# A round of the down projection by seven products for eight, in the middle of the second SwiGLU block

## The chip, the cores and the metric

The kernel runs on one core of a Trainium2 chip. The metric is the device time of one execution in microseconds; of several runs the median counts. A core has a matrix engine (TensorE, PE in the profile), a vector engine (VectorE, DVE), a scalar engine (ScalarE, ACT), GpSimd (POOL), an engine that here only issues transfers (SyncE, SP), and DMA queues. TensorE accumulates into eight PSUM banks; the other engines take results out of them.

## The reference

One decoder layer for 512 tokens of 1024 channels: a SwiGLU block, a mixing block (attention, convolution and memory side by side), and a second SwiGLU block. The change concerns the second SwiGLU block:

```python
def swiglu(x, w_gate, w_up, w_down):
    return (jax.nn.silu(x @ w_gate) * (x @ w_up)) @ w_down
...
        x = x + 0.5 * swiglu(rms_norm(x, g_ffn1[l]), w_ffn1_gate[l], w_ffn1_up[l], w_ffn1_down[l])
...
        x = x + 0.5 * swiglu(rms_norm(x, g_ffn2[l]), w_ffn2_gate[l], w_ffn2_up[l], w_ffn2_down[l])
    return x
```

The hidden width is 2816, which is 22 tiles of 128. Everything is float32.

## The kernel before

**Layout and precision.** x stays in SBUF, turned, as eight pieces [128 channels, 512 tokens]; `x[:, d]` is piece d. Each operand is split into a rounded high part and the rest (hi and lo), and each product is the sum of three matmuls, hi by hi, hi by lo and lo by hi. The high part of a weight is cast by ScalarE (L214, L208), the low part is a subtraction on VectorE (L219, L209).

**A SwiGLU block.** It runs over 22 hidden tiles f. The first few (four in block 1, three in block 2) use plain products; the others use `fast`, which computes the gate and the up projection of a tile by a scheme of seven products instead of eight on halves of 256 tokens: seven blocks of 12 matmuls 128x256, 84 in all, with sums of weights made by VectorE (`make_sums`, L160 to L163) and sums of results made by ScalarE (copies out of PSUM) and VectorE. The gate's sum is at L629, its Silu on ScalarE at L630, the up sum at L640 and their product at L644.

**Rounds of the down projection.** The hidden tiles are gathered in rounds, and each round's contribution is added to x while later tiles are computed. In block 2 the rounds are tiles 0 to 2, 3 to 6, 7 to 10, 11 to 14, 15 to 17 and 18 to 21 (`PLANS`). Round 3, tiles 11 to 14, is spread over tiles 15 to 18: each of them gets one load of down weights and two steps of `down` for two pieces of x, 24 matmuls of 128x256 each, accumulated into x by VectorE at L671. The first step stands ahead of the product B_T4 of `fast`, the second behind the tile's hidden result. The last round, tiles 18 to 21, is done behind tile 21 by `seven(g)`, g = 0 to 3, each for two pieces of x: seven products of six matmuls instead of eight. It needs three parts of a weight as they are, four sums of quarters (`four`, L147 to L150), and sums of the hidden tiles by pairs (`paired`). `seven` leaves its results by L529 (a scaled sum of PSUM and x, then a transfer to the output); half sums of products go through ScalarE (`half`, L515) into s12 and s45, which are added to x by VectorE (L519) or by a GpSimd transfer that accumulates (L521).

**Weights.** `Weights` keeps a list of loads and a list of items to split. Raw loads of 512 KB go through four buffers (wraw) on SP's queue, each issued as soon as the split of the last item that reads the old content of its buffer is done; split weights go through four buffers (w0 to w3), a tile's last item through vhi and vlo. `W.next()` gives the next item and splits up to three ahead.

**What sets the order.** The program order below is given to a scheduler, which orders each engine's instructions by its own estimates of their times; only the last stage (`seven`) keeps the written order. TensorE, ScalarE and VectorE each run their list in order and wait on semaphores. PSUM banks: four `mm`, two `sc`, two `tp`. Work tiles `t`: five; `sum` tiles: three.

Of the kernel before, what the change touches and what calls it, by code (L numbers as in the profile page):

```python
# [85 lines left out]
class Weights:  # L86
# [36 lines left out]
    def add_seven(self, ap, off):  # L123
# [116 lines left out]
class Plan:  # L240
# [12 lines left out]
    def steps(self, f):  # L253

        first, second, third = self.rounds[:3]
        if f < first[1]:
            return [], [], []
        if f < second[1]:
            early = self.loads(0) if self.direct < 4 else self.loads(0)[:-1]
            late = self.loads(0)[len(early) :]  # L260
            return early if f == second[0] else [], late if f == second[0] + 1 else [], []
        queue = [d for q in range(1, self.last) for d in self.loads(q)]
        i = f - third[0]
        if f < NF - 1:
            return [], [queue[i]], []
        return ([], [], queue[i:]) if self.seven else ([], [queue[i]], queue[i + 1 :])


PLANS = {
    1: Plan([(0, 4), (4, 8), (8, 12), (12, 16), (16, 18), (18, 22)], 4, False),  # L270
    2: Plan([(0, 3), (3, 7), (7, 11), (11, 15), (15, 18), (18, 22)], 3, True),
}


def layer(tc, ctx, a):
# [35 lines left out]
    def ffn_weights(n, memory):  # L311
        gu, plan = a[f"wgu{n}"], PLANS[n]

        def down(r, g):
            lo, hi = plan.rounds[r]
            m = plan.per_load(r)
            return a[f"wd{n}"][g * m : (g + 1) * m, :, lo:hi].rearrange("d p k m -> p d (k m)")

        for f in range(NF):
            pre, mid, post = plan.steps(f)  # L320
            for d in pre:
                W.add(down(*d), OTHER if d[0] else WIDE, n == 2 and d[0] == 0)
            if f < plan.direct:
                for i in range(2):
                    W.add(flat(gu[f, i]), WIDE, n == 2 and f > 1)
            else:
                W.add_pair(flat(gu[f, 0]), flat(gu[f, 1]), [(down(*d), OTHER if d[0] else WIDE) for d in mid])
            for d in post:
                W.add(down(*d), OTHER if d[0] else WIDE)
            if memory and f == MEM_F:  # L330
                for t in range(2):
                    W.add(flat(a["wmk"][t]), HALF)
                for c in range(2):
                    W.add(flat(a["wmv"][:, 4 * c : 4 * c + 4]), TURNED)
        r = plan.last
        for g in range(KT // plan.per_load(r)):
            (W.add_seven if plan.seven else W.add)(down(r, g), (HALF, OTHER)[g % 2])

    ffn_weights(1, True)
    for t in range(12):  # L340
# [120 lines left out]
    def ffn(pool, norm, first, gain, hooks, next_gain, last):  # L461
# [3 lines left out]
        W.extra = pool  # L465
        bh, bl = {}, {}

        even, sevens, later = {}, [], []

        def halves(t):  # L470
            hi, lo = (both := atile("h7"))[:, :256], both[:, 256:]
# [4 lines left out]
        def paired(f, t):  # L476

            l, r = t[:, :256], t[:, 256:]
            if not (f - plan.rounds[-1][0]) % 2:
                even[f] = l, r, halves(l)  # L480
                return
            el, er, first = even[f - 1]
            m = pool.tile([P, 4, 256], F32, tag="sum", name=nm("h7"), bufs=SUM_BUFS)
            t1, t2, t3, t4 = (m[:, i] for i in range(4))
            out = [first, halves(l)]
            DVE.tensor_tensor(t1, er, el, op=ALU.subtract)
            out.append(halves(t1))
            DVE.tensor_tensor(t2, r, t1, op=ALU.subtract)
# [6 lines left out]
            sevens.append(out)  # L495

        def seven(g):

# [7 lines left out]
            def prod(ps, w, at, step, block, first):  # L506
                for q in range(2):
                    hi, lo = sevens[q][block]
                    s = slice(at + q * step, at + q * step + P)
                    PE.matmul(ps, w[0][:, s], hi, start=first and q == 0, stop=False, skip_group_check=not first)  # L510
                    PE.matmul(ps, w[0][:, s], lo, start=False, stop=False, skip_group_check=not first)
                    PE.matmul(ps, w[1][:, s], hi, start=False, stop=q == 1, skip_group_check=not first)

            def half(to, ps, sign=1):
                ACT.activation(to, ps, AF.Copy, scale=0.5 * sign)  # L515

            def add(to, part):
                if g > 1:
                    DVE.tensor_tensor(to, to, part, op=ALU.add)  # L519
                else:  # L520
                    POOL.dma_start(to, part, accum_op=ALU.add)  # L521

            def leave(d, t, ps):
                o = work()[:, : t.stop - t.start]
                xd = x[:, d, t]
                if ps.shape[-1] < t.stop - t.start:
                    o, xd = (v.rearrange("p (a b) -> p a b", a=2) for v in (o, xd))
                    ps = ps.unsqueeze(1).to_broadcast([P, 2, 256])
                DVE.scalar_tensor_tensor(o, ps, 0.5, xd, op0=ALU.mult, op1=ALU.add)  # L529
                if len(o.shape) == 3:  # L530
                    o = o.rearrange("p a b -> p (a b)")
# [3 lines left out]
            if g < 2:  # L535
                W.four(W.items[W.at + 4][0])
            wa, ws = W.next(), W.next()
            prod(b, wa, 0, 256, H_11, True)
            half(s12[:, l], b)
            prod(de[:, l], wa, 128, 256, H_21, True)  # L540
            prod(de[:, r], ws, 0, 128, H_T1, True)
            half(s45[:, r], de[:, r])
            while later:
                leave(*later.pop(0))
            prod(b, ws, 256, 128, H_T2, False)
            half(s12[:, r], b)
            add(x0, s12)
            prod(c, wa, 512, 128, H_T4, True)
            half(s45[:, l], c, -1)
            add(x1, s45)  # L550
            W.split_to(W.at + 3)
            prod(de[:, r], ws, 768, 128, H_22, False)
            prod(b, ws, 512, 128, H_T3, False)
            whole = slice(0, T)
            if end:
                leave(2 * g, whole, de)
                leave(2 * g + 1, l, b)
                leave(2 * g + 1, r, b)
            else:
                later.extend([(2 * g + 1, whole, b), (2 * g, whole, de)])  # L560

        def hidden(f, t):
            if plan.seven and f >= plan.rounds[-1][0]:
                paired(f, t)
                return
            h_hi[f], h_lo[f] = atile("hh"), atile("hl")
# [46 lines left out]
        def fast(f, mid):  # L613
# [14 lines left out]
            product(de[:, r], w2, 0, B_22, False)  # L628
            DVE.tensor_tensor(g, de, s12, op=ALU.add)  # L629
            ACT.activation(g, g, AF.Silu)  # L630
# [86 lines left out]
            for hook in hooks.get(f, ()):  # L717
                hook()
        r = plan.last
        if plan.seven:  # L720
# [683 lines left out]
```

## Time and profile before

| | us |
|---|---|
| median of 3 runs | 861.53 (861.43 to 861.96) |
| profiled execution | 861.62 |
| span of the profile | 859.8 |
| granted TensorE clock | 1.0 |
| in_wgu load, issue to landing, median | 3.6 |
| GpSimd accumulating transfer x<-s, 256 KB | 3.8 |

The span runs from the first to the last instruction of the profiled execution; its own time is longer by what lies around it. The page's second part gives the busy share in 40 slices, tenths per slice, 21.5 us each; the second block fills the last fifteen or so:

```profile
PE   8999999999999999999999999999999999999997
DVE  7998977877868897869989985899787878787896
...
DMA  7335334333453434222010323863334342323325
```

TensorE is busy in nearly all of every slice, VectorE in six to nine tenths, the transfers in one to seven.

### The profile page before, as it was taken

To read this page: it belongs to the slowest core of one execution; us is meant where nothing else is said; L and a number is where in the kernel's file an instruction comes from. 1 tells how busy PE (TensorE), PEld (TensorE's weight loads), DVE (VectorE), ACT (ScalarE), POOL (GpSimd) and SP (SyncE) were. 2 spreads that over 40 slices of the span, in tenths; PEclk is the share of its full clock that TensorE was granted. 3 is DMA by queue.
4 is the path that set the end of the run, shared out by engine and by line. 5 is a ranking of instruction groups with operands and counts; after the bars stand their busy time and mean duration, and the time that the engine had idled before them with its cause. 6 is when DMAs were issued, how large, how long until landed. Compare 5 with 4: busy or idle time off the path is not lost. (4 is left out here: it accounts for less than half of the span.)

```text
span 859.8 us, 15853 instructions
## 1 busy us (share of the span) xinstructions
PE 850.1 (99%) x6397; PEld 788.6 (92%) x6397; DVE 708.9 (82%) x1208; ACT 466.3 (54%) x792; POOL 37.4 (4%) x40
## 2 busy tenths in 40 slices
PE   8999999999999999999999999999999999999997
PEld 5889999999999999988676788889999999999997
DVE  7998977877868897869989985899787878787896
ACT  7465555455654444633948764656554544545554
POOL 0000000000000000300000022120000000000001
PEclk9999999999999999999999999999999999999999
DMA  7335334333453434222010323863334342323325
GB/s 274 123 91 149 105 98 125 98 119 127 129 157 120 123 111 130 74 98 62 13 32 31 113 97 100 178 141 122 123 98 124 99 123 86 114 96 103 95 75 148
DMA packets 36795, 95.13 MB, mean 111 GB/s; under 512 B 3441, under 2 KB 8049, under 8 KB 36721
## 3 DMA queue, kind: packets, MB, share of 16 engines
q1 hardware_dynamic: 32032, 85.99, 32.1%
q0 software_dynamic: 3536, 6.55, 4.6%
q10 hardware_dynamic: 1152, 1.57, 0.6%
q8 instruction: 50, 0.82, 0.4%
q14 instruction: 25, 0.20, 0.1%
HBM read 88.07 MB, written 2.10 MB: 105 GB/s over the span
## 5 line engine op out<-in xcount | busy, mean ns | idle before, releaser
L609 PE MATMUL mm<-bh,w 128*128 128x256 f32 x888 | 245.5, 276 | 0.4 <-ACT kept L624 0.4
L610 PE MATMUL mm<-bl,w 128*128 128x256 f32 x888 | 245.2, 276 | 0.0
L611 PE MATMUL mm<-bh,w 128*128 128x256 f32 x888 | 245.2, 276 | 0.0
L609 PEld LDWEIGHTS mm<-bh,w 128*128 128x128 f32 x888 | 166.7, 188 | 0.8 <-ACT kept L624 0.6
L415 PE MATMUL mm<-hl,w 128*128 128x256 f32 (+1 forms) x584 | 167.3, 287 | 0.0
L416 PE MATMUL mm<-hh,w 128*128 128x256 f32 (+1 forms) x584 | 167.2, 287 | 0.0
L414 PE MATMUL mm<-hh,w 128*128 128x256 f32 (+1 forms) x584 | 167.0, 287 | 0.0
L610 PEld LDWEIGHTS mm<-bl,w 128*128 128x128 f32 x888 | 166.7, 188 | 0.1
L611 PEld LDWEIGHTS mm<-bh,w 128*128 128x128 f32 x888 | 166.7, 188 | 0.0
L214 ACT CAST w<-wraw 128x1024 fp32r<-128x1024 f32 (+2 forms) x119 | 119.1, 1005 | 74.8 <-PE mm L611 23.7
L219 DVE TENSOR_TENSOR w<-wraw,w 128x1024 fp32r<-128x1024 f32 (+2 forms) x113 | 132.5, 1176 | 29.9 <-ACT w L214 26.4
L219 DVE TENSOR_TENSOR w<-s,w 128x1024 fp32r<-128x1024 f32 x78 | 95.3, 1222 | 40.3 <-PE mm L611 34.5
L414 PEld LDWEIGHTS mm<-hh,w 128*128 128x128 f32 x584 | 109.6, 188 | 2.4 <-ACT hh L567 0.3
L415 PEld LDWEIGHTS mm<-hl,w 128*128 128x128 f32 x584 | 109.6, 188 | 2.2
L416 PEld LDWEIGHTS mm<-hh,w 128*128 128x128 f32 x584 | 109.6, 188 | 2.1
L214 ACT CAST w<-s 128x1024 fp32r<-128x1024 f32 x78 | 81.9, 1052 | 27.1 <-PE mm L611 20.4
L414 PE MATMUL mm<-xh,w 128*128 128x512 f32 x176 | 69.7, 401 | 0.5 <-ACT xh L425 0.4
L415 PE MATMUL mm<-xl,w 128*128 128x512 f32 x176 | 69.4, 394 | 0.6 <-DVE xl L426 0.5
L416 PE MATMUL mm<-xh,w 128*128 128x512 f32 x176 | 69.1, 393 | 0.0
L630 ACT ACTIVATE t<-t 128x512 f32<-128x512 f32 x37 | 23.4, 633 | 68.3 <-DVE t L629 68.3
L671 DVE SCALAR_TENSOR_TENSOR x<-mm,x 128x512 f32<-128x512 f32 x80 | 54.2, 683 | 2.0 <-PE mm L416 2.0
L214 ACT CAST vhi<-wraw 128x512 fp32r<-128x512 f32 x37 | 23.0, 621 | 42.7 <-PE sc L610 34.7
(290 smaller groups left out, 1496.8 us busy)
## 6 DMA issues: line engine op xcount, KB each, us to landing
wraw<-in_wgu SPq DMA_DIRECT2D x86, 512.0 KB, 3.6
wraw<-in_wd SPq DMA_DIRECT2D x38, 512.0 KB, 3.6
wraw<-in_win SPq DMA_DIRECT2D x12, 512.0 KB, 3.5
wraw<-in_wd SPq DMA_DIRECT2D x8, 384.0 KB, 3.3
x<-t POOLq DMA_DIRECT2D x8, 256.0 KB, 4.1
out<-t SPq DMA_DIRECT2D x7, 256.0 KB, 2.3
x<-in_xT SPq DMA_DIRECT2D x3, 512.0 KB, 6.8
wraw<-in_wout_a SPq DMA_DIRECT2D x6, 256.0 KB, 2.7
```

Source lines behind the costliest of these rows:

```text
L214: nc.scalar.copy(hi[:, :cols], raw[:, :cols])
L219: nc.vector.tensor_tensor(lo[:, :cols], raw[:, :cols], hi[:, :cols].bitcast(F32), op=ALU.subtract)
L414: PE.matmul(ps[:, t], wh[:, w], hi(k)[:, t], start=one, stop=False, skip_group_check=cut > 1)
L415: PE.matmul(ps[:, t], wh[:, w], lo(k)[:, t], start=False, stop=False, skip_group_check=cut > 1)
L416: PE.matmul(ps[:, t], wl[:, w], hi(k)[:, t], start=False, stop=end, skip_group_check=cut > 1)
L609: PE.matmul(ps, wh[:, c], bh[k][:, block], start=one, stop=False, skip_group_check=not first)
L610: PE.matmul(ps, wh[:, c], bl[k][:, block], start=False, stop=False, skip_group_check=not first)
L611: PE.matmul(ps, wl[:, c], bh[k][:, block], start=False, stop=end, skip_group_check=not first)
L630: ACT.activation(g, g, AF.Silu)
L671: DVE.scalar_tensor_tensor(o, ps, 0.5, xd, op0=ALU.mult, op1=ALU.add)
```

## The change

Round 3 of block 2 is done by seven products too. `Plan.seven` becomes a tuple of rounds. In tiles 15 to 18 the two `down` steps are replaced by `inside(n, g)`: its first part (`begin`: H_11, H_21, H_T1, 18 matmuls) stands where the first step stood, its second (`end`: H_T2, H_T4, H_22, H_T3, 24 matmuls) behind the hidden result. VectorE adds two results to x from PSUM, and GpSimd issues two transfers that add s12 and s45. The load of 512 KB stays, but becomes two items (three parts; four sums). The hidden tiles 11 to 14 go through `paired`, in which the halves of the even tile are now made with the odd tile. In `fast`, in both blocks, the product B_T3, the second use of the third weight, moves ahead of the first down step and of B_T4. In `seven` the additions for g = 1 go to VectorE, and the last pair (g = 3) is written in another order, with H_21 in a bank of its own.

```diff
@@ add_pair @@
-        for ap, off in mid:
-            self.add(ap, off)
+        for ap, off, seven in mid:
+            (self.add_seven if seven else self.add)(ap, off)
@@ PLANS @@
-    2: Plan([(0, 3), (3, 7), (7, 11), (11, 15), (15, 18), (18, 22)], 3, True),
+    2: Plan([(0, 3), (3, 7), (7, 11), (11, 15), (15, 18), (18, 22)], 3, (3, 5)),
@@ paired @@
-            if not (f - plan.rounds[-1][0]) % 2:
-                even[f] = l, r, halves(l)
+            n = seven_at[f]
+            if not (f - plan.rounds[n][0]) % 2:
+                even[f] = l, r
                 return
-            el, er, first = even[f - 1]
+            el, er = even[f - 1]
...
-            out = [first, halves(l)]
+            out = [halves(el), halves(l)]
@@ new, with product7, half and twice moved out of seven @@
+        def inside(n, g):
+            l, r = slice(0, 256), slice(256, 512)
+            b, de = mm_bank()[:, l], mm_bank()
+            c = sc_bank()[:, l]
+            s12, s45 = work(), work()
+            x0, x1 = x[:, 2 * g], x[:, 2 * g + 1]
+            wa, ws = W.next(), W.next()
+            def begin():
+                product7(b, wa, 0, 256, H_11, True, n)
+                half(s12[:, l], b)
+                product7(de[:, l], wa, 128, 256, H_21, True, n)
+                product7(de[:, r], ws, 0, 128, H_T1, True, n)
+                half(s45[:, r], de[:, r])
+            def end():
+                product7(b, ws, 256, 128, H_T2, False, n)
+                half(s12[:, r], b)
+                product7(c, wa, 512, 128, H_T4, True, n)
+                half(s45[:, l], c, -1)
+                product7(de[:, r], ws, 768, 128, H_22, False, n)
+                product7(b, ws, 512, 128, H_T3, False, n)
+                DVE.scalar_tensor_tensor(x0, de, 0.5, x0, op0=ALU.mult, op1=ALU.add)
+                x2 = x1.rearrange("p (a b) -> p a b", a=2)
+                DVE.scalar_tensor_tensor(x2, twice(b), 0.5, x2, op0=ALU.mult, op1=ALU.add)
+                POOL.dma_start(x0, s12, accum_op=ALU.add)
+                POOL.dma_start(x1, s45, accum_op=ALU.add)
+            return [begin, end]
@@ seven, add @@
-                if g > 1:
+                if g > 0:
                     DVE.tensor_tensor(to, to, part, op=ALU.add)
@@ seven, g = 3 alone (p2: H_21 into bank e; p4: H_T4; p7: H_T3; p3: H_22) @@
             prod(b, wa, 0, 256, H_11, True)
             half(s12[:, l], b)
             prod(de[:, r], ws, 0, 128, H_T1, True)
             half(s45[:, r], de[:, r])
             while later:
                 leave(*later.pop(0))
+            p4()
             prod(b, ws, 256, 128, H_T2, False)
             half(s12[:, r], b)
             add(x0, s12)
+            p2()
+            leave(2 * g, l, e)
+            p7()
+            leave(2 * g + 1, whole, b)
+            p3()
+            leave(2 * g, r, de[:, r])
@@ fast @@
             ACT.activation(g, g, AF.Silu)
+            product(b, w2, 512, B_T3, False)
             rest = []
             for d in mid:
-                rest += down(*d)
+                rest += (inside if d[0] in plan.seven else down)(*d)
             if rest:
                 rest.pop(0)()
             w3 = W.next()
             product(c, w3, 0, B_T4, True)
             ACT.copy(s45[:, l], c)
-            product(b, w2, 512, B_T3, False)
```

The names in the following rows are numbered by load and item: wraw146 is the 146th load, w207 the 207th item, s12 and s43 the sums of two neighbouring loads (gate and up of one tile), s7 the four sums of a down load, t the gate and up sums. On VectorE, at the gate's sum of tile 16 of block 2, there stands before:

```order
L219 TENSOR_TENSOR w206_8536<-wraw142_8356,w206_8536 128x1024
L219 TENSOR_TENSOR w207_8561<-s12_142_8555,w207_8561 128x1024
L629 TENSOR_TENSOR t_788_8474<-mm_784_8470,kept_786_8472 128x512
L160 TENSOR_TENSOR s12_145_8738<-wraw146_8564 128x512
L163 TENSOR_TENSOR s43_145_8739<-wraw145_8539,wraw146_8564 128x512
L161 TENSOR_TENSOR s12_145_8738<-wraw145_8539,s12_145_8738 128x512
L671 SCALAR_TENSOR_TENSOR x_69<-mm_790_8566,x_69 128x512
```

and with the change, at the same place:

```order
L688 TENSOR_TENSOR t_799_8523<-mm_795_8519,kept_797_8521 128x512
L219 TENSOR_TENSOR w208_8626<-wraw142_8433,w208_8626 128x1024
L148 TENSOR_TENSOR s7_144_8754<-s7_144_8754,wraw144_8530 128x256
L149 TENSOR_TENSOR s7_144_8754<-wraw144_8530,s7_144_8754 128x256
L219 TENSOR_TENSOR w209_8637<-s12_142_8631,w209_8637 128x1024
L160 TENSOR_TENSOR s12_145_8827<-wraw146_8640 128x512
L699 TENSOR_TENSOR t_800_8524<-kept_798_8522,mm_794_8518 128x512
L219 TENSOR_TENSOR vlo213_8788<-wraw143_8444,vhi213_8787 128x512
L703 TENSOR_TENSOR t_800_8524<-t_800_8524,t_799_8523 128x512
```

wraw142 and wraw146 use the same buffer. The split that frees it (w206 before, w208 now) stood ahead of the split of s12 and of the gate's sum, and now stands behind the gate's sum (L688); L160, the first sum of wraw146, stands three places behind that split before and four places behind it now.

On ScalarE, from the gate's Silu of the same tile on, there stands before:

```order
L630 ACTIVATE t_788_8474<-t_788_8474 128x512
L214 CAST vhi210_8689<-wraw143_8381 128x512
L638 COPY kept_787_8473<-sc_785_8471 128x256
L214 CAST w208_8592<-s43_142_8556 128x1024
L567 CAST hh_791_8622<-t_789_8475 128x512
```

and now:

```order
L689 ACTIVATE t_799_8523<-t_799_8523 128x512
L214 CAST w209_8637<-s12_142_8631 128x1024
L508 ACTIVATE t_804_8624<-mm_801_8621 128x256
L508 ACTIVATE t_805_8625<-mm_802_8622 128x256
L214 CAST vhi213_8787<-wraw143_8444 128x512
```

The half sums that read the products of `inside` out of PSUM (L508) stand behind the Silu and the cast of the sum s12; before, the cast of that sum stood ahead of the Silu.

On VectorE, the last nine operations before:

```order
L519 TENSOR_TENSOR x_69<-x_69,s12_874_9761 128x512
L519 TENSOR_TENSOR x_69<-x_69,s45_875_9762 128x512
L529 SCALAR_TENSOR_TENSOR t_883_9845<-tp_871_9758,x_69 128x512
L529 SCALAR_TENSOR_TENSOR t_884_9848<-tp_872_9759,x_69 128x512
L519 TENSOR_TENSOR x_69<-x_69,kept_881_9823 128x512
L519 TENSOR_TENSOR x_69<-x_69,t_882_9824 128x512
L529 SCALAR_TENSOR_TENSOR t_885_9879<-mm_879_9821,x_69 128x512
L529 SCALAR_TENSOR_TENSOR t_886_9882<-mm_878_9820,x_69 128x256
L529 SCALAR_TENSOR_TENSOR t_887_9885<-mm_878_9820,x_69 128x256
```

and now:

```order
L558 TENSOR_TENSOR x_69<-x_69,s12_894_9849 128x512
L558 TENSOR_TENSOR x_69<-x_69,s45_895_9850 128x512
L568 SCALAR_TENSOR_TENSOR t_904_9928<-tp_891_9846,x_69 128x512
L568 SCALAR_TENSOR_TENSOR t_905_9931<-tp_892_9847,x_69 128x512
L558 TENSOR_TENSOR x_69<-x_69,t_902_9912 128x512
L558 TENSOR_TENSOR x_69<-x_69,kept_901_9911 128x512
L568 SCALAR_TENSOR_TENSOR t_906_9956<-mm_903_9913,x_69 128x256
L568 SCALAR_TENSOR_TENSOR t_907_9965<-mm_898_9908,x_69 128x512
L568 SCALAR_TENSOR_TENSOR t_908_9974<-mm_899_9909,x_69 128x256
```

Before, three results (one of 512, two of 256) stood together at the end; now the left half, the whole piece and the right half stand one behind the other, each for another product.

More of the change, by code (lines that the diff above doesn't have):

```diff
@@ L326, in ffn_weights @@
             else:
-                W.add_pair(flat(gu[f, 0]), flat(gu[f, 1]), [(down(*d), OTHER if d[0] else WIDE) for d in mid])
+                W.add_pair(flat(gu[f, 0]), flat(gu[f, 1]), [(down(*d), OTHER if d[0] else WIDE, d[0] in plan.seven) for d in mid])
             for d in post:
@@ L336, in ffn_weights @@
         for g in range(KT // plan.per_load(r)):
-            (W.add_seven if plan.seven else W.add)(down(r, g), (HALF, OTHER)[g % 2])
+            (W.add_seven if r in plan.seven else W.add)(down(r, g), (HALF, OTHER)[g % 2])
     ffn_weights(1, True)
@@ L466, in ffn @@
         bh, bl = {}, {}
-        even, sevens, later = {}, [], []
+        even, sevens, later = {}, {r: [] for r in plan.seven}, []
+        seven_at = {f: r for r in plan.seven for f in range(*plan.rounds[r])}
         def halves(t):
@@ L494, in paired, with product7, half, twice @@
             out.append(halves(r))
-            sevens.append(out)
+            sevens[n].append(out)
+        def product7(ps, w, at, step, block, first, n):
+            for q in range(2):
+                hi, lo = sevens[n][q][block]
+                s = slice(at + q * step, at + q * step + P)
+                PE.matmul(ps, w[0][:, s], hi, start=first and q == 0, stop=False, skip_group_check=not first)
+                PE.matmul(ps, w[0][:, s], lo, start=False, stop=False, skip_group_check=not first)
+                PE.matmul(ps, w[1][:, s], hi, start=False, stop=q == 1, skip_group_check=not first)
+        def half(to, ps, sign=1):
+            ACT.activation(to, ps, AF.Copy, scale=0.5 * sign)
+        def twice(ps):
+            return ps.unsqueeze(1).to_broadcast([P, 2, 256])
+        def inside(n, g):
[24 more added lines that the diff above has]
+            return [begin, end]
         def seven(g):
@@ L504, in seven, with prod @@
             x0, x1 = x[:, 2 * g], x[:, 2 * g + 1]
[L506 to L515, printed above, removed]
+            def prod(*args):
+                product7(*args, plan.last)
             def add(to, part):
-                if g > 1:
+                if g > 0:
                     DVE.tensor_tensor(to, to, part, op=ALU.add)
@@ L537, in seven, with p2, p4, p3 @@
             wa, ws = W.next(), W.next()
+            whole = slice(0, T)
+            e = bank()[:, l] if end else de[:, l]
+            def p2():
+                prod(e, wa, 128, 256, H_21, True)
+            def p4():
+                prod(c, wa, 512, 128, H_T4, True)
+                half(s45[:, l], c, -1)
+                add(x1, s45)
+            def p3():
+                prod(de[:, r], ws, 768, 128, H_22, False)
+            def p7():
+                prod(b, ws, 512, 128, H_T3, False)
             prod(b, wa, 0, 256, H_11, True)
             half(s12[:, l], b)
-            prod(de[:, l], wa, 128, 256, H_21, True)
+            if not end:
+                p2()
             prod(de[:, r], ws, 0, 128, H_T1, True)
@@ L547, in seven @@
             add(x0, s12)
[L548 to L559, printed above, removed]
-                later.extend([(2 * g + 1, whole, b), (2 * g, whole, de)])
+            if not end:
+                p4()
+                W.split_to(W.at + 3)
+                p3()
+                p7()
+                later.extend([(2 * g + 1, whole, b), (2 * g, whole, de)])
+                return
+            p2()
+            leave(2 * g, l, e)
+            p7()
+            leave(2 * g + 1, whole, b)
+            p3()
+            leave(2 * g, r, de[:, r])
         def hidden(f, t):
-            if plan.seven and f >= plan.rounds[-1][0]:
+            if f in seven_at:
                 paired(f, t)
```

9 lines of the change are left out of this document (5 added, 4 removed).

## The prediction

> **What bounds the kernel now.** I read the page's totals first, then TensorE's timeline, then the table by windows for the tiles that change, and last the list of waits.
>
> ```profile
> span 859.8 us, 15853 instructions
> PE 850.1 (99%) x6397; PEld 788.6 (92%) x6397; DVE 708.9 (82%) x1208; ACT 466.3 (54%) x792; POOL 37.4 (4%) x40
> ...
> 740.00:760.00 20.00, 20.00 (x179) 20.00 (x178) 16.48 (x24) 9.74 (x16) 0.00 (x0) 1.00 0.28 82
> ...
> sum 80.00, PE 80.00 PEld 80.00 DVE 61.82 ACT 40.00 POOL 0.00; mean PE 20.00 PEld 20.00 DVE 15.46 ACT 10.00 POOL 0.00
> ...
> PE mm L609 <- ACT kept L624: 0.4, 1, 0.4
> ```
>
> The window rows give PE, weight loads, VectorE, ScalarE and GpSimd busy, then the granted clock (1.00). From 700 to 780 us, tiles 13 to 18 of the second block, TensorE is never idle; the longest wait of a product of these tiles on anything is one of 0.4 us in the whole run. So in this block the number of matmuls sets the time, and a removed matmul is worth one step of TensorE's pace:
>
> ```profile
> 700.97 0.28 PE L609 MATMUL mm<-bh,w 128*128 128x256 f32 x1
> ...
> 706.07 0.28 PE L609 MATMUL mm<-bh,w 128*128 128x256 f32 x1
> ```
>
> Between these two starts stand 45 matmuls of 128x256: 5.10 / 45 = 0.1133 us each. (The 0.28 us of a row is its latency; they overlap.)
>
> VectorE is the engine with least room behind it: 61.82 of 80 us. A tile is 84 matmuls of gate and up plus 48 of the down round, 132 x 0.1133 = 14.96 us, so VectorE works 61.82 / 80 x 14.96 = 11.6 us in it.
>
> **Term 1, products removed: -2.72 us.** In tiles 15 to 18 two plain down steps (48 matmuls) become seven products of 6 (42). Six fewer in four tiles are 24 x 0.1133 = 2.72 us. A tile becomes 126 x 0.1133 = 14.28 us. This holds only if TensorE stays fed.
>
> **Term 2, the end: -1.15 us.** The last product and what VectorE does behind it now:
>
> ```profile
> 854.53 0.28 PE L512 MATMUL mm<-h,w 128*128 128x256 f32 x1
> ...
> 850.08 1.29 DVE L529 SCALAR_TENSOR_TENSOR t<-mm,x 128x512 f32<-128x512 f32 x2 [2.30 <-DMA x<-s]
> 851.28 1.28 DVE L519 TENSOR_TENSOR x<-x,s 128x512 f32<-128x512 f32 x2
> 852.66 1.29 DVE L529 SCALAR_TENSOR_TENSOR t<-tp,x 128x512 f32<-128x512 f32 x2
> 853.87 0.69 DVE L519 TENSOR_TENSOR x<-x,kept 128x512 f32<-128x512 f32 x1
> 854.47 0.69 DVE L519 TENSOR_TENSOR x<-x,t 128x512 f32<-128x512 f32 x1
> 855.07 1.35 DVE L529 SCALAR_TENSOR_TENSOR t<-mm,x 128x512 f32<-128x512 f32 x3
> ...
> out<-t SPq DMA_DIRECT2D x7, 256.0 KB, 2.3
> out<-t SPq DMA_DIRECT2D x2, 128.0 KB, 1.9
> ```
>
> The last matmul ends at 854.81, VectorE at 856.42, 1.61 us later, because it is backed up: it stood 2.30 us at 850.08 for an accumulating transfer and has run without a break since. The row of x3 is one 512 and two 256 operations. With g=1 added by VectorE the transfer it waited for is gone, so the 1.2 us of two more additions (851.28 to 852.66 is the pair's price, 1.28) fit into the 2.30 us that go. With the last pair reordered, the two sums of the pair before and both additions are due ahead of the last three products (18 matmuls, 2.04 us), the sums that leave follow product by product, and behind the last product stands one operation of 256. I put it 0.1 us behind the last matmul's end (an estimate) and give it the 0.42 us of a 256 operation below, so VectorE ends 0.5 us behind TensorE instead of 1.61: -1.1, and a little less queue ahead of the last 128 KB transfer: -1.15. Bounds: 0, if the output transfers (2.3 and 1.9 us) queue up instead, and -1.4.
>
> **Term 3, VectorE in tiles 15 to 18: +2.2 us.** The added operations have these rows (from the last stage, where the same sums are made):
>
> ```profile
> 842.84 0.42 DVE L147 TENSOR_TENSOR s<-wraw 128x256 f32<-128x256 f32 x1
> 843.29 0.42 DVE L148 TENSOR_TENSOR s<-s,wraw 128x256 f32<-128x256 f32 x1
> 843.75 0.42 DVE L149 TENSOR_TENSOR s<-wraw,s 128x256 f32<-128x256 f32 x1
> 844.09 0.42 DVE L150 TENSOR_TENSOR s<-wraw 128x256 f32<-128x256 f32 x1
> ...
> 845.62 1.02 DVE L209 TENSOR_TENSOR w<-wraw,w 128x512 fp32r<-128x512 f32 x2
> 846.56 1.22 DVE L219 TENSOR_TENSOR w<-s,w 128x1024 fp32r<-128x1024 f32 x1
> ```
>
> Start to start: 0.45 + 0.46 + 0.34 + 0.33 = 1.58 for the four sums and 0.94 for the split in two parts. The split of 1024 takes the place of the plain one, and the two accumulations into x stay two. So VectorE's work in a tile goes from 11.6 to 11.6 + 1.58 + 0.94 = 14.1, in a tile of 14.28. That alone would just fit. What doesn't is a wait that the order moves into it:
>
> ```profile
> 732.45 0.38 ACT L620 COPY kept<-mm 128x256 f32<-128x256 f32 x1 [0.27 <-PE mm L611]
> ...
> 734.93 1.23 DVE L219 TENSOR_TENSOR w<-wraw,w 128x1024 fp32r<-128x1024 f32 x1 [1.49 <-ACT w L214]
> 737.88 1.23 DVE L219 TENSOR_TENSOR w<-s,w 128x1024 fp32r<-128x1024 f32 x1 [1.72 <-PE mm L611]
> 739.02 0.68 DVE L629 TENSOR_TENSOR t<-mm,kept 128x512 f32<-128x512 f32 x1
> 739.86 0.69 DVE L160 TENSOR_TENSOR s<-wraw 128x512 f32<-128x512 f32 x1 [0.15 <-DMA wraw<-in_wgu]
> 740.47 0.69 DVE L163 TENSOR_TENSOR s<-wraw,wraw 128x512 f32<-128x512 f32 x1
> 741.07 0.69 DVE L161 TENSOR_TENSOR s<-wraw,s 128x512 f32<-128x512 f32 x1
> ...
> 736.19 0.33 SPq L178 DMA_DIRECT2D wraw<-in_wgu  x1
> ...
> DMA to landing us min/median/max: 3.2/3.5/3.7
> ```
>
> The split at 734.93 is the last reader of a gate weight; it ends at 736.16, and at 736.19 the load of the next up weight goes into the same buffer. The first sum of that weight (739.86) starts 3.70 us after the split's end, as soon as it has landed. Now 3.55 us of that are other waits and work; the load costs 0.15 us. In the new order this split stands behind the gate's sum (L688), and between it and the first sum stand only two small sums and one split: 0.46 + 0.34 + 1.14 (737.88 to 739.02, start to start) = about 2.0 us. The rest, 3.6 - 2.0 = 1.6 us, VectorE stands still, with the up product's operations queued behind. Its period is then 14.1 + 1.6 = 15.7 if the additions cost all of their price, and 15.3 by a sum over pitches (0.60 for each operation of 512, as from 740.47 to 741.07, 1.14 for each of 1024: 13.7); I take 15.4.
>
> What TensorE waits for is further on: the gate's sum releases the Silu on ScalarE, behind which stand a cast of 1024 and then the half sum that reads the first product (H_11) out of its bank; only then may H_T2 go into that bank.
>
> ```profile
> 739.74 0.63 ACT L630 ACTIVATE t<-t 128x512 f32<-128x512 f32 x1 [1.90 <-DVE t L629]
> ...
> 743.38 1.05 ACT L214 CAST w<-s 128x1024 fp32r<-128x1024 f32 x1 [0.59 <-PE mm L611]
> ```
>
> From the gate's sum to the Silu 0.72, then 0.63, 1.05 and 0.38 for the half (as the copy at 732.45), less some overlap of 0.1: 2.65 us. H_T2 is the 103rd matmul of its tile: 102 x 0.1133 = 11.56 us in. So the gate's sum may start up to 8.9 us into a tile. In tile 15 it starts now at 739.02, in a tile that starts at about 730.9 (732.45 less the first 12 matmuls of 1.36 and the 0.2 us to the copy): 8.1. The split of 737.88 goes behind it, so I take 7.8, an estimate. The slack is 1.1; in each of three steps from tile to tile VectorE falls back 15.4 - 14.28 = 1.12. TensorE stands for 3 x 1.12 - 1.1 = 2.26; **2.2** in the sum. Bounds: 0, if the load lands in time, to 4.2 at a period of 16.05 (the longest landing shown, 3.7, and the additions at their full time, 0.42 x 4 and 1.02).
>
> **Costed at nothing.** The product B_T3 ahead in both blocks: it frees the third weight's buffer a few us sooner, but no wait of TensorE is on that buffer; the up sum comes about 0.8 us later, and its bank is needed by the next tile's second product, 1.36 us into it. If that cover went in all 37 such tiles (18 and 19 in the two blocks) at some tenths each, it would be up to 10 us, far from the nearest row, a single wait of 0.4. The halves of h moved to the odd tile, and eleven operations of 256 in tiles 12 and 14 instead of two of 512: about 2.8 us of VectorE per pair, inside 18.18 us of idle time from 700 to 780 (80 - 61.82). Without that room it is part of term 3. The 8 added transfers that accumulate into x:
>
> ```profile
> 839.20 1.74 POOL L521 DMA_DIRECT2D x<-s  x2 [271.60 <-DVE s L148]
> ...
> 839.00 0.43 DVE L149 TENSOR_TENSOR s<-wraw,s 128x256 f32<-128x256 f32 x1
> 839.34 0.42 DVE L150 TENSOR_TENSOR s<-wraw 128x256 f32<-128x256 f32 x1
> ```
>
> GpSimd has nothing else there (0.00 in the windows), and the next round comes to the same part of x two tiles later at the soonest. Each issue takes 1.74 / 2 = 0.87 us on GpSimd.
>
> The Trainium skill ("SBUF — State Buffer", section "SBUF: two separate sides") says that VectorE and GpSimd share a pair of ports that is locked for a whole instruction, also by a VectorE operation with two inputs in SBUF against a GpSimd operation that reads it. By that rule VectorE could stand for 1.74 us in each of these tiles. The rows speak against it for this kind of GpSimd work: beside the issue at 839.20 the VectorE operation of 839.34, two inputs in SBUF, took 0.42 us as at 844.09. It stays a rival.
>
> **The sum.** 861.62 (the profiled execution, 1.8 over its span) - 2.72 - 1.15 + 2.2 = 859.95; the median is 0.09 below that execution: **859.9 us**.
>
> **Rivals.**
> 1. VectorE keeps up: the load lands in time because the scheduled order leaves VectorE waiting elsewhere, as it does now for 3.55 us. Term 3 is 0 to 0.8: 861.5 - 3.9 = 857.6 to 858.4. For it: 14.1 fits into 14.28. Against: the order row itself.
> 2. Slower: VectorE's loop with the load is longer. It decides where 3 x (p - 14.28) - 1.1 is over 3.87 + 1.72, at a period p of 16.5, 1.1 above mine: landing of 4.7 instead of 3.6, or the same lost twice in the round. At 16.7 it is 6.2, 863.8. Against: no landing here over 3.7.
> 3. The GpSimd issues hold VectorE for their 1.74 us: p = 17.1, term 3 is 7.4, 865.0.
> 4. The end gains nothing, since the output transfers bound it: 861.0.
> 5. The change takes no product off TensorE's path. The order shows 24 matmuls fewer, so this gets no chance of its own.
>
> **How the numbers follow.** Forecast (859.0 to 860.6) 0.45; rival 1 0.25; between them and the slower side (term 3 of 3 to 5, or rival 4) 0.18; rival 2 0.09; rival 3 0.03. The range leaves out the ends: 857.5 to 862.0. Within 0.2% (1.72 us, about what a measurement of this kernel tells from no change) lies 859.8 to 863.25. The forecast stands on that border, and I split it: faster 0.25 + 0.22 = 0.47; same 0.23 + 0.18 = 0.41; slower 0.12.
>
> **What would show it.** Term 1: TensorE at 126 matmuls in a tile of 15 to 18 and the same 0.1133. Term 3: the first sum of an up weight (L160) in tiles 16 and 17 waiting about 1.6 us for its load, and idle time of TensorE ahead of H_T2 (L510) from tile 16 on, growing to some 2.2 us in all; no such idle time is rival 1, more than 5 us is rival 2. Rival 3: VectorE operations of over a microsecond beside a GpSimd issue. Term 2: VectorE ends 0.5 us behind the last matmul. I am wrong if TensorE gets gaps in tiles 4 to 14 or in block 1, where I cost the moved product at nothing.

## The result, and the profile after

| | before | changed |
|---|---|---|
| median of 5 runs, us | 861.96 (861.43 to 862.31) | 868.97 (868.18 to 870.76) |
| ratio | | 1.0088, 95% interval 1.0075 to 1.0102 |
| span of the profile, us | 859.8 | 866.9 |
| matmuls | 6397 | 6373 |
| start of the last matmul, us | 854.53 | 862.77 |

The change made the kernel 7 us slower; 859.9 us had been forecast, in a range of 857.5 to 862.0. The 24 matmuls are gone and the end behind the last matmul is shorter, but TensorE, which hardly waited before, waits. The page's totals and the costliest group of the changed kernel (the last two columns of the group are the idle time of TensorE ahead of it and what ended it; L668 is L609 of before):

```profile
span 866.9 us, 15868 instructions
...
PE 853.2 (98%) x6373; PEld 788.8 (91%) x6373; DVE 727.2 (84%) x1252; ACT 468.7 (54%) x826; POOL 42.5 (5%) x46
...
L668 PE MATMUL mm<-bh,w 128*128 128x256 f32 x888 | 247.2, 278 | 5.5 <-ACT kept L679 2.2
```

The same windows as in the prediction, of the changed kernel:

```profile
740.00:760.00 20.00, 20.00 (x179) 20.00 (x178) 18.46 (x30) 11.59 (x22) 1.74 (x2) 1.00 0.50 129
...
800.00:820.00 20.00, 16.84 (x143) 16.25 (x142) 17.05 (x29) 9.48 (x18) 1.12 (x2) 1.00 0.47 121
```

In tiles 15 to 18 TensorE is nearly full and VectorE fuller than before (18.46 us of 20, it was 16.48). From 800 to 820 us, tiles 19 and 20, where the round by seven products is over, TensorE stands for 3 us. (Tiles are counted by TensorE's rows, 84 matmuls of gate and up in each.) Where the time went by stage, worked out from the starts of TensorE's rows in each trace. A block is taken from the first to the last matmul of `fast` in it; the last stage is what follows, up to the start of the last matmul:

| us | block 1 | between | block 2 | last stage |
|---|---|---|---|---|
| before | 262.75 | 239.63 | 254.93 | 27.20 |
| changed | 266.16 | 241.13 | 258.57 | 27.31 |
| with B_T3 back | 262.75 | 239.80 | 253.87 | 27.31 |
| B_T3 moved alone | 266.26 | 241.44 | 257.07 | 27.20 |

Block 1, in which the change moves nothing but one product, is 3.4 us longer. Block 2 is 3.6 us longer though 2.72 us of matmuls are gone: 6.4 us of new waits. The 1.5 us between the blocks are something else. In this trace the clock granted to TensorE fell to about half from 460 to 464 us, while it worked without a pause (the clock is the third number from the end of a row):

```profile
461.00:462.00 1.00, 1.00 (x5) 0.40 (x3) 1.00 (x9) 1.00 (x4) 0.00 (x0) 0.50 0.39 129
```

The traces of three other versions show the same, somewhere from 456 to 464 us, one of them with B_T3 at its old place. In these four the stretch between the blocks takes 240.7 to 241.4 us, in the other thirteen 239.3 to 240.3. So nothing shows that this part comes from the change.

What TensorE waits for in the blocks shows at a seam, the end of one tile and the start of the next. One in block 1 of the changed kernel, its VectorE, ScalarE and TensorE rows in order:

```profile
196.52 1.23 DVE L219 TENSOR_TENSOR w<-s,w 128x1024 fp32r<-128x1024 f32 x1 [0.91 <-PE mm L670]
197.67 0.68 DVE L688 TENSOR_TENSOR t<-mm,kept 128x512 f32<-128x512 f32 x1
200.72 0.69 DVE L160 TENSOR_TENSOR s<-wraw 128x512 f32<-128x512 f32 x1 [2.37 <-DMA wraw<-in_wgu]
201.33 0.68 DVE L163 TENSOR_TENSOR s<-wraw,wraw 128x512 f32<-128x512 f32 x1
201.93 1.22 DVE L219 TENSOR_TENSOR w<-s,w 128x1024 fp32r<-128x1024 f32 x1
...
205.47 0.68 DVE L699 TENSOR_TENSOR t<-kept,mm 128x512 f32<-128x512 f32 x1
206.19 0.69 DVE L703 TENSOR_TENSOR t<-t,t 128x512 f32<-128x512 f32 x1
...
202.43 0.36 ACT L698 COPY kept<-sc 128x256 f32<-128x256 f32 x1
...
206.91 0.62 ACT L626 CAST hh<-t 128x512 fp32r<-128x512 f32 x1 [2.94 <-DVE t L703]
207.44 1.04 ACT L214 CAST w<-wraw 128x1024 fp32r<-128x1024 f32 x1
208.39 0.91 ACT L828 ACTIVATE mh<-t,par 128x256 fp32r<-128x256 f32 x2
209.20 0.35 ACT L679 COPY kept<-mm 128x256 f32<-128x256 f32 x1
...
209.60 0.39 PE L668 MATMUL mm<-bh,w 128*128 128x256 f32 x1 [0.87 <-ACT kept L679]
```

Read it from below. TensorE waits 0.87 us for L679, the copy of the new tile's first product out of its bank. L679 stands in ScalarE's queue behind the cast of the old tile's hidden result (L626), which waited 2.94 us for VectorE's product of gate and up (L703). The copy that the up sum (L699) needs was done at 202.79, yet the up sum starts at 205.47: VectorE had stood 2.37 us for a load (L160) and had put a split of 1.22 us (201.93) in front of the up sum. The same tile before:

```profile
196.56 0.68 DVE L629 TENSOR_TENSOR t<-mm,kept 128x512 f32<-128x512 f32 x1
198.01 0.69 DVE L160 TENSOR_TENSOR s<-wraw 128x512 f32<-128x512 f32 x1 [0.77 <-DMA wraw<-in_wgu]
...
202.34 0.69 DVE L644 TENSOR_TENSOR t<-t,t 128x512 f32<-128x512 f32 x1
202.95 1.22 DVE L219 TENSOR_TENSOR w<-s,w 128x1024 fp32r<-128x1024 f32 x1
```

There the split stands behind the product of gate and up, and the wait for the load is 0.77 us: 5.8 us from the gate's sum to the product, and now 8.5. This is one of the worse tiles. The mean from the gate's sum to the product is 5.2 us before and 6.6 in the changed kernel over the 18 tiles of `fast` in block 1, and 5.0 and 6.6 over the 19 of block 2.

L160 stands between the gate's and the up sum here in both kernels. What it meets differs: the two loads of a tile are issued when VectorE's splits free their buffers, and the splits are late. The issues of that tile, before and then with the change:

```profile
191.42 2.63 SPq L178 DMA_DIRECT2D wraw<-in_wgu  x2
```

```profile
194.43 1.54 SPq L178 DMA_DIRECT2D wraw<-in_wgu  x2
```

The second load was issued 2.3 us behind the first before and 1.2 us now. It landed 4.2 us after its issue before and 5.1 us now.

The list of waits has it as a sum over the run; of before, then of the changed kernel:

```profile
ACT hh L567 <- DVE t L644: 25.9, 28, 2.2
DVE s L160 <- DMA wraw<-in_wgu: 23.2, 24, 2.2
```

```profile
ACT hh L626 <- DVE t L703: 63.6, 27, 4.4
DVE s L160 <- DMA wraw<-in_wgu: 42.2, 28, 2.9
```

### The profile page after: what moved, and what is told of

The parts are those of the page before. It is cut to its first block, busy times and chain, and to the rows that moved or that the text cites. A ratio compares the mean times of both kernels' runs of the same rounds, so it can differ in the third digit from the quotient of the medians.

```text
span 866.9 us, 15868 instructions
## 1 busy us (share of the span) xinstructions
PE 853.2 (98%) x6373; PEld 788.8 (91%) x6373; DVE 727.2 (84%) x1252; ACT 468.7 (54%) x826; POOL 42.5 (5%) x46
## 5 line engine op out<-in xcount | busy, mean ns | idle before, releaser
L668 PE MATMUL mm<-bh,w 128*128 128x256 f32 x888 | 247.2, 278 | 5.5 <-ACT kept L679 2.2
L668 PEld LDWEIGHTS mm<-bh,w 128*128 128x128 f32 x888 | 166.7, 188 | 8.1 <-ACT kept L679 3.3
L415 PE MATMUL mm<-hl,w 128*128 128x256 f32 (+1 forms) x520 | 149.6, 288 | 0.0
L416 PE MATMUL mm<-hh,w 128*128 128x256 f32 (+1 forms) x520 | 149.6, 288 | 0.0
L414 PE MATMUL mm<-hh,w 128*128 128x256 f32 (+1 forms) x520 | 149.4, 289 | 0.0
L214 ACT CAST w<-wraw 128x1024 fp32r<-128x1024 f32 (+2 forms) x115 | 114.8, 1003 | 57.8 <-issue 27.4
L219 DVE TENSOR_TENSOR w<-wraw,w 128x1024 fp32r<-128x1024 f32 (+2 forms) x109 | 127.9, 1176 | 17.4 <-ACT w L214 13.6
L219 DVE TENSOR_TENSOR w<-s,w 128x1024 fp32r<-128x1024 f32 x82 | 100.2, 1222 | 25.9 <-PE mm L670 16.9
L214 ACT CAST w<-s 128x1024 fp32r<-128x1024 f32 x82 | 86.0, 1050 | 44.8 <-PE mm L670 36.4
L414 PEld LDWEIGHTS mm<-hh,w 128*128 128x128 f32 x520 | 97.6, 188 | 2.4 <-ACT hh L626 0.3
L416 PEld LDWEIGHTS mm<-hh,w 128*128 128x128 f32 x520 | 97.6, 188 | 2.2
L415 PEld LDWEIGHTS mm<-hl,w 128*128 128x128 f32 x520 | 97.6, 188 | 2.2
L160 DVE TENSOR_TENSOR s<-wraw 128x512 f32<-128x512 f32 x37 | 25.6, 691 | 42.3 <-DMA wraw<-in_wgu 42.2
L626 ACT CAST hh<-t 128x512 fp32r<-128x512 f32 x29 | 18.0, 622 | 63.6 <-DVE t L703 63.6
```

The source lines that it names most:

```text
L160: nc.vector.tensor_tensor(s12[:, l], u[:, l], u[:, r], op=ALU.add)
L214: nc.scalar.copy(hi[:, :cols], raw[:, :cols])
L219: nc.vector.tensor_tensor(lo[:, :cols], raw[:, :cols], hi[:, :cols].bitcast(F32), op=ALU.subtract)
L414: PE.matmul(ps[:, t], wh[:, w], hi(k)[:, t], start=one, stop=False, skip_group_check=cut > 1)
L415: PE.matmul(ps[:, t], wh[:, w], lo(k)[:, t], start=False, stop=False, skip_group_check=cut > 1)
L416: PE.matmul(ps[:, t], wl[:, w], hi(k)[:, t], start=False, stop=end, skip_group_check=cut > 1)
```

## The experiments

All ratios are to the kernel before, run beside each on the same chip. Its median was 861.8 to 862.8 us from one set of runs to the next, so versions are compared by these ratios.

**The parts of the change, one by one.** First the changed kernel with B_T3 back, then B_T3 moved alone:

```diff
             ACT.activation(g, g, AF.Silu)
-            product(b, w2, 512, B_T3, False)
...
             product(c, w3, 0, B_T4, True)
             ACT.copy(s45[:, l], c)
+            product(b, w2, 512, B_T3, False)
```

> The changed kernel with the product B_T3 back behind B_T4, everything else of the change kept. Theory A (the moved product costs most): the gaps of TensorE at the seams of tiles in block 1 (about 3.3 us) and with them some 1 us in the mixing block go, and of the 4.2 us in tiles 19 to 21 at least half: 859 to 862 us. Theory B (the round by seven products overloads VectorE, and the moved product is harmless, as the prediction had it): the gaps in tiles 19 to 21 stay, 867 to 869 us, with at most what block 1 loses by itself gone, 864.

Measured: 859.38 us, ratio 0.9970 (0.9959 to 0.9981).

> The kernel before with the product B_T3 moved, nothing else. Theory A: 865 to 868 us, with gaps ahead of the second product of a tile in both blocks. Theory B: 861.5 to 862.5 us, the prediction's nothing.

The edit is the diff above turned round, in the kernel before. Measured: 868.19 us, 1.0071 (1.0056 to 1.0085). Theory A holds. Without the moved product the change gains 2.6 us; the moved product alone loses 6.1 us. The two together cost more than their sum: in the whole change the product makes 10.2 us of difference. Some 4 us thus belong to both together. In the blocks' table 2.6 us of that are in block 2, where the product makes 4.7 us of difference in the whole change and 2.1 alone.

> The last stage of the changed kernel alone (additions of g = 1 on VectorE, last pair reordered, and the halves of tiles 18 and 20 made a tile later), round 3 plain, B_T3 at its old place. Both theories: the prediction's second term, 860.4 us, with the last vector operation 0.5 us behind the last matmul.

```diff
-    2: Plan(..., 3, (3, 5)),
+    2: Plan(..., 3, (5,)),
```

with B_T3 back. Measured: 861.09 us, 0.9992 (0.9983 to 1.0001): in the direction expected, 0.7 us, and not clear of nothing. In its trace VectorE ends 0.49 us behind the last matmul, as expected.

> Round 3 by seven products alone (with the halves made a tile later), B_T3 and the last stage as before. Theory A: 24 matmuls less and 0 to 2.2 us of new waits, 859 to 861.5 us. Theory B: 864 to 866 us, the gaps of tiles 19 to 21 as in the changed kernel.

The changed kernel with B_T3 back and `seven` as before. Measured: 860.61 us, 0.9984 (0.9975 to 0.9993), inside theory A's range.

**What the moved product does.** It ends the use of the third weight's buffer before B_T4 instead of behind it. The cast and split of the next tile's third weight go into that buffer, so the scheduler could now put them ahead of the up sum, as the seam above shows. In the next two runs the split is emitted behind the product of gate and up and pinned there on VectorE:

```diff
+            W.conv_ahead -= 1
             w3 = W.next()
+            W.conv_ahead += 1
...
             DVE.tensor_tensor(u, u, g, op=ALU.mult)
+            W.pin = tc.keep_in_program_order
+            W.split_to(W.at + W.conv_ahead)
+            W.pin = lambda ins: ins
             hidden(f, u)
@@ split_to @@
-                    nc.vector.tensor_tensor(lo[:, :cols], raw[:, :cols], hi[:, :cols].bitcast(F32), op=ALU.subtract)
+                    self.pin(nc.vector.tensor_tensor(lo[:, :cols], raw[:, :cols], hi[:, :cols].bitcast(F32), op=ALU.subtract))
```

> The kernel before with B_T3 moved, and on VectorE the split of the next tile's third weight (w<-s43) held behind the up sum and its product with the gate, where it stands in the kernel before. Theory C (the moved product frees the third weight's buffer early, the scheduler then puts that split, 1.2 us, ahead of the up sum, and this delay is the whole loss): 861.5 to 863 us. Rival D (the move hurts by itself: by the up sum's new last input, or by the loads that follow each other more closely): 866 to 869 us as with the move alone.

Measured: 864.62 us, 1.0021 (1.0010 to 1.0033): between the two; 4.3 of the 6.1 us that the move costs by these ratios are back.

> The changed kernel whole, with the same split held behind the up sum. Theory C: 858.5 to 861 us, as with B_T3 back. Rival D: 866 to 869 us. If the seven products alone make the loads late in tiles 15 to 18: 862 to 865 us.

Measured: 864.20 us, 1.0021 (1.0009 to 1.0033): not Theory C's range but that of the third case. Holding the split gives back 5.8 of 7.6 us, not all. How much of it block 1 gets is not settled by the two traces: with the same order of block 1 on TensorE, VectorE and ScalarE, it took 266.21 us in the one with B_T3 alone, as without the held split (266.26), and 263.77 us in the one of the whole change. L160 still stands between the gate's and the up sum and waits for its load. It does so in the changed kernel too, in tile 15 (736.0 to 750.3 us by TensorE's rows):

```profile
746.25 1.22 DVE L219 TENSOR_TENSOR w<-s,w 128x1024 fp32r<-128x1024 f32 x1
748.98 0.69 DVE L160 TENSOR_TENSOR s<-wraw 128x512 f32<-128x512 f32 x1 [1.51 <-DMA wraw<-in_wgu]
749.59 0.68 DVE L699 TENSOR_TENSOR t<-kept,mm 128x512 f32<-128x512 f32 x1
```

So the sums of an up weight were made from the start of a tile instead, with L160 pinned behind what the tile before left on VectorE:

```diff
             w0 = W.next()
+            W.sums_early(tc.keep_in_program_order)
...
+    def sums_early(self, keep):
+        if self.after and (i := min(self.after)) < self.loaded:
+            self.keep = keep
+            self.after.pop(i)()
+            self.keep = lambda ins: ins
```

> The changed kernel whole, with two places on VectorE set as with B_T3 back: the split of the third weight behind the up sum, and the first sum of the following pair's up weight (L160, made from the start of a tile and held behind what the tile before left) instead of between the gate's and the up sum. Theory F (these two places are the whole loss of the moved product): 858.5 to 860.5 us. Rival D (the move hurts in another way as well): 862 to 865 us, as with the split alone.

Measured, with this edit and the one on the split: 862.24 us, 1.0004 (0.9995 to 1.0013). That is rival D's range: Theory F missed.

> The changed kernel whole, with the second of the two places alone (L160 from the start of a tile). Theory F: part of the loss, 860 to 865 us, since in block 1 the third weight's split still stands ahead of the up sum; the waits for a load between the gate's and the up sum go. Rival (the loads have no part in it): 866 us or more.

Measured, with the sums' place alone: 862.83 us, 1.0010 (1.0001 to 1.0019).

So this place alone gives back 6.7 us, the split alone 5.8 and both 7.2: each undoes most of the same loss, and their shares can't be told apart. With the sums made early, the same seam of block 1 looks like this (its line numbers are a little further: L220 is the split, L707 the up sum, L633 the cast of the hidden result):

```profile
198.13 1.23 DVE L220 TENSOR_TENSOR w<-s,w 128x1024 fp32r<-128x1024 f32 x1 [0.67 <-ACT w L215]
...
202.28 0.68 DVE L707 TENSOR_TENSOR t<-kept,mm 128x512 f32<-128x512 f32 x1
...
203.71 0.62 ACT L633 CAST hh<-t 128x512 fp32r<-128x512 f32 x1 [0.62 <-DVE t L711]
```

The split (198.13) still stands ahead of the up sum (202.28), but VectorE no longer waits for a load between the two sums, and block 1 takes 262.96 us, nearly as before. This fits a loop, argued from the rows and not tested apart: late splits issue the loads late, L160 waits longer for them, and that makes the next splits late.

The two places leave the whole change nearly 3 us behind the version with B_T3 back. Whether that rest is the product's or comes from elsewhere is told by B_T3 alone with both places:

> The kernel before with B_T3 moved, and both places on VectorE set right (the third weight's split behind the up sum, L160 from the start of a tile). If these two places are all that the move costs: 861.5 to 862.7 us. If the move hurts in a further way: 864 us or more.

Measured: 862.72 us, 1.0004 (0.9995 to 1.0013). Setting the two places takes away what the move costs, to within 1.1 us. It may also take away something that the kernel before has, since L160 stands between the two sums there as well and waits 23.2 us for loads in all; the kernel before with L160 early and nothing else was not run. Part of the rest in the whole change is another wait: with the sums earlier, TensorE waits three times, from 744 to 788 us, for ScalarE's cast of a weight of that round. The longest such wait in the whole change with both places:

```profile
744.79 0.39 PE L511 MATMUL mm<-h,w 128*128 128x256 f32 x1 [0.74 <-ACT w L216]
```

**By which way a late up sum reaches TensorE.** The first attempt only called `hidden` a tile later:

```diff
             DVE.tensor_tensor(u, u, g, op=ALU.mult)
-            hidden(f, u)
+            waiting.append((f, u))
...
             ACT.copy(s12[:, r], b)
+            if waiting:
+                hidden(*waiting.pop(0))
```

> The changed kernel whole, but a tile's hidden result is cast and split one tile later, behind the second copy out of PSUM of the next tile, so that on ScalarE nothing that waits for the up sum stands ahead of those copies. Theory E (TensorE loses its time because ScalarE waits in its queue for the hidden result, with the next tile's first copy behind): the gaps at the seams go though VectorE is as late as before: 859 to 863 us. Rival (TensorE waits for VectorE through PSUM banks, or ScalarE isn't on the path): 866 us or more.

Measured: 868.28 us, 1.0067 (1.0054 to 1.0079). It says nothing of the theory: the scheduler put the casts back ahead of the copies.

> B_T3 back behind B_T4 and the hidden results a tile later. Theory E: the 1.3 us that TensorE still loses in tile 20 with B_T3 back go, 857.5 to 859 us. Rival: 859.4 us or more, as with B_T3 back alone.

Measured: 858.94 us, 0.9961 (0.9947 to 0.9975), with one gap left in tile 20, 1.1 us by the starts of TensorE's rows. The casts (`hi` and `h_hi`) were then pinned on ScalarE, behind the second copy:

```diff
+                pin[0] = tc.keep_in_program_order
                 hidden(*waiting.pop(0))
+                pin[0] = lambda ins: ins
...
-            ACT.copy(h_hi[f], t)
+            pin[0](ACT.copy(h_hi[f], t))
```

> The changed kernel whole; on ScalarE the casts of a tile's hidden result are held behind the second copy out of PSUM of the next tile (in the earlier attempt the scheduler had put them ahead again). Theory E (the way from a late up sum to TensorE is ScalarE's queue): 860 to 863 us with VectorE as late as before. Rival: 866 us or more.

Measured: 860.84 us, 0.9987 (0.9978 to 0.9996). VectorE is as late as in the changed kernel (from the gate's sum to the product of gate and up 7.0 us on the mean of the 18 tiles of block 1, 6.6 in the changed kernel, 5.2 before), yet by the ratios 8.7 of the 10.2 us between the changed kernel and the one with B_T3 back are regained. ScalarE at a seam in that run:

```profile
193.72 0.37 ACT L686 COPY kept<-mm 128x256 f32<-128x256 f32 x1 [0.92 <-PE mm L671]
193.99 0.63 ACT L627 CAST hh<-t 128x512 fp32r<-128x512 f32 x1
...
204.59 0.37 ACT L680 COPY kept<-mm 128x256 f32<-128x256 f32 x1 [0.31 <-PE mm L671]
```

The cast (L627) waits for nothing, and the first copy (L680) waits 0.31 us for TensorE instead of TensorE for it. The rival's way, through a PSUM bank, has a small part too. In tile 20 of this run TensorE waits for VectorE's addition of a down product into x, as it does for 0.67 us in the changed kernel:

```profile
805.40 0.38 PE L669 MATMUL mm<-bh,w 128*128 128x256 f32 x1 [0.68 <-DVE x L737]
```

> The kernel before with B_T3 moved, and on ScalarE the casts of the hidden result held behind the second copy of the next tile. If ScalarE's queue is the only way from the late up sum to TensorE: 861 to 862.5 us. If there is a second way: 864 us or more.

Measured: 862.96 us, 1.0003 (0.9994 to 1.0011), against 1.0071 without the held casts: with B_T3 moved alone, ScalarE's queue is by far the main way. The next run says how much room is left for another.

> The kernel before with the casts held behind the second copy of the next tile, nothing else. Its only gap in block 2 (0.5 us, tile 3) goes: 861.2 us against 861.8; so nearly all that the version with B_T3 back and held casts gains comes from the seven products and the last stage. Rival: the held casts alone are worth 2 us or more.

Measured: 861.60 us, 0.9990 (0.9981 to 0.9999): 0.9 us by itself. (By the count of TensorE's rows the gap is in tile 7, which the expectations call tile 3.) Against this run the one with B_T3 moved and the casts held is still 1.1 us slower, hardly clear of the noise, so a second way worth about 1 us is not excluded.

> B_T3 back, and on ScalarE the casts held behind the second copy of the next tile. Theory E: the gaps of TensorE in tiles 3 and 20 go, 857.5 to 859 us. Rival: 859.4 us or more.

Measured: 858.51 us, 0.9957 (0.9943 to 0.9971), the best of all, faster than both kernels. Its span and two windows (the first is around tile 16 and shows VectorE full, the second is tiles 20 and 21):

```profile
span 854.7 us, 15878 instructions
...
740.00:760.00 20.00, 20.00 (x178) 20.00 (x178) 19.86 (x32) 14.13 (x26) 1.74 (x2) 1.00 0.62 160
...
800.00:820.00 20.00, 20.00 (x179) 20.00 (x178) 19.93 (x36) 11.64 (x24) 0.00 (x0) 1.00 0.40 118
```

TensorE has no idle time there at all, beside a VectorE that is 99% busy. Block 2 takes 251.70 us by the trace: 254.93 less the 2.72 of the matmuls and 0.5 of the one gap that was there before. What moving the product costs with the casts held in both is 2.6 us by the ratios (0.9987 against 0.9957), so the queue is most of the way and not all of it.

## Why the prediction was wrong

- **The step that failed is the one costed at nothing, B_T3 ahead in both blocks.** It said that no wait of TensorE is on the third weight's buffer, and looked no further. TensorE's wait wasn't the question: an earlier free buffer lets the scheduler start what fills it earlier, and that is a split of 1.2 us on the engine that makes the up sum. With L160, which stands ahead of the up sum and meets a later load, it makes the product of gate and up 1.4 us later on the mean of block 1's tiles and 1.6 on block 2's. Alone: +0.7%, 6 us. The prediction named its own sign of this, gaps in block 1, and they came; none of its rivals had the moved product in it. The prediction had even a price for a lost cover, up to 10 us, and set it aside because of a single wait of 0.4 us; that wait, of TensorE on ScalarE's copy (L624), was the same mechanism in small, since the cast L567 had waited 1.07 us for VectorE ahead of that copy. It bounded nothing.
- **The delay of the up sum was given as 0.8 us from its last input.** The input was there in time (202.79 above); the delay is VectorE's own queue. And the cover was looked for at the bank of the up sum, while the main way to TensorE is the cast of the hidden result in ScalarE's queue.
- **Term 1 holds**: 24 matmuls fewer, and TensorE's pace unchanged. With B_T3 back, TensorE has no gap of over 0.2 us in tiles 15 to 18.
- **Term 2 holds.** From the last matmul's start to the end of the span: 5.29 us before, 4.12 in the changed kernel, 1.17 less (predicted 1.15). The end of the changed kernel:

```profile
862.77 0.28 PE L505 MATMUL mm<-h,w 128*128 128x256 f32 x1
...
861.41 0.68 DVE L558 TENSOR_TENSOR x<-x,kept 128x512 f32<-128x512 f32 x1
862.18 1.35 DVE L568 SCALAR_TENSOR_TENSOR t<-mm,x 128x256 f32<-128x256 f32 x3
```

  VectorE ends at 863.53, 0.48 us behind the last matmul's end at 863.05; 0.5 was said. As a time of whole runs the last stage alone gave 0.7 us, not clear of nothing.
- **Term 3 had the right wait and the wrong effect.** L160 waits 1.51, 1.74 and 1.46 us for its load in tiles 15 to 17 (1.6 was worked out). Rival 2 was held off by the longest landing shown, 3.7 us; from 700 us on it is 5.2 us in the changed kernel, and yet TensorE loses little in these tiles. (The chain given as 2.65 us, from the gate's sum on, adds up to 2.68; nothing hangs on it.) TensorE's idle time ahead of H_T2, which was to grow to 2.2 us, is this one row:

```profile
776.54 0.39 PE L503 MATMUL mm<-h,w 128*128 128x256 f32 x1 [0.22 <-ACT t L508]
```

  And the place of L160 comes from the moved product, not from the round by seven products: with B_T3 back the scheduler puts it at the start of the next tile, VectorE is busy 19.53 of 20 us (13.9 in a tile of 14.28, where 14.1 was said), and TensorE doesn't wait there (rival 1), by that run's windows:

```profile
740.00:760.00 20.00, 20.00 (x179) 20.00 (x178) 19.53 (x32) 13.97 (x26) 1.74 (x2) 1.00 0.61 159
```

  What is lost then, 1.3 us, is in tile 20, at the same seam through ScalarE, because the casts of the pair 18 and 19 stand ahead of the copies.
- **Rival 3 is out.** Beside GpSimd's issues VectorE keeps its times:

```profile
754.94 1.14 POOL L540 DMA_DIRECT2D x<-t  x1
...
755.26 0.68 DVE L161 TENSOR_TENSOR s<-wraw,s 128x512 f32<-128x512 f32 x1
755.86 1.21 DVE L219 TENSOR_TENSOR w<-s,w 128x1024 fp32r<-128x1024 f32 x1
```

  The lock that the Trainium skill describes ("SBUF — State Buffer", section "SBUF: two separate sides") doesn't show for these issues, two-input operations of VectorE in SBUF included. The prediction's own comparison was weaker than it reads: its row of 844.09 stands beside an issue of GpSimd too, that of 843.96.
- Without the step that failed the sum would have been close: 861.96 - 2.72 - 1.15 + 1.3 = 859.4 us, and 859.38 was measured with B_T3 back. But the 1.3 in it is measured and not forecast. With the prediction's own 2.2 the sum is 860.3, and that it comes near is partly luck: its 2.2 stood for a wait in other tiles, by another way.

One thing stays open: why the moved product costs 10.2 us in the whole change and 6.1 alone. Of the 4.7 us in block 2, 3.1 are in tiles 19 and 20. There L160 meets its longest wait for a load (2.9 us, in tile 19), and TensorE waits behind the late casts for two copies (0.99 and 1.51 us) and for VectorE (0.34 and 0.67 us). How the two parts of the change add up to this was not followed.

## What to carry to other kernels

Freeing a buffer earlier isn't free where a scheduler fills it: what refills it also needs an engine, and it may be put ahead of work that is due sooner. Before costing a moved instruction at nothing, compare every engine's order at a plain place that the change isn't about, and follow the late result through each in-order queue up to the engine that sets the time. Operations that wait for a late result should not stand in a queue ahead of the copies that release TensorE (held back here, they took most of the loss away with VectorE as late as in the changed kernel).

## What was not expected of the hardware

In the whole change with the split held behind the up sum, TensorE stood 2.07 us in tile 20 of the trace, and then its clock was halved for some 3 us (the wait, then windows, with the granted clock as the third number from the end of a row):

```profile
812.57 0.38 PE L669 MATMUL mm<-bh,w 128*128 128x256 f32 x1 [2.07 <-ACT kept L684]
...
805.00:812.00 7.00, 5.50 (x47) 5.20 (x46) 6.96 (x14) 3.81 (x9) 0.00 (x0) 1.00 0.20 59
...
813.00:814.00 1.00, 1.00 (x7) 1.00 (x7) 1.00 (x3) 0.73 (x1) 0.00 (x0) 0.50 0.40 63
814.00:815.00 1.00, 1.00 (x6) 1.00 (x6) 1.00 (x2) 0.00 (x0) 0.00 (x0) 0.50 0.89 327
```

A matmul took 0.213 us there instead of 0.113. In the changed kernel the longest such wait was 1.51 us, and the clock stayed at 1.00 there. The Trainium skill ("TensorE: Matmul & The Clock Gate", section "HAM oscillation — how this bites in real kernels") warns of idle gaps of over some 3.4 us; here the halving came right behind one of 2.07 us, with 5.5 us of work in the 7 us up to 812. This is one case and sets no threshold. The halving between the blocks shown above (460 to 464 us of the changed kernel) came without such a gap: by its rows TensorE has no idle time in the 40 us ahead of it, in the mixing block. What set it off is not shown.
